# A weight-split feed-forward pair on one core: first sums issued a slab earlier, at least two product jobs between tiles of the one tile bank, column norm six quads later

## The chip, the cores and the metric

The kernel runs on one core of a Trainium2 chip, in one launch. The metric is the time of one execution in device microseconds (us); three runs were made, and the median counts. The engines of the core are TensorE (PE, with its weight loads as PEld), VectorE (DVE), ScalarE (ACT), GpSimd (POOL) and SyncE (SP), which issues most of the DMAs.

## The reference

A decoder trunk of two layers on 256 tokens of width 2048, all in float32: a layer that mixes by causal pooling, a layer of differential attention, memory cross-attention in both, and after each mixer a feed-forward part. The change lies in the two feed-forward parts alone:

```python
def squared_relu_mlp(h, w1, w2):
    z = jax.nn.relu(h @ w1)
    return (z * z) @ w2
...
x = x + squared_relu_mlp(rms_norm(x, ffn_norm[i]), w_ff1[i], w_ff2[i])
```

`w_ff1` is 2048 x 8192 and `w_ff2` 8192 x 2048.

## The kernel before, in words

**Splits.** Every weight comes from HBM as float32 and is split on chip into a high part `hi_ring` (a cast on ScalarE, L171) and a low part `lo_ring` (a subtraction on VectorE, L172); TensorE multiplies the parts and adds the products. The two rings have six slots of 512 columns. Weights in ordinary order come in *quads* of four 128x128 blocks (job N, one slot). One DMA, `raw` (L133), brings two quads.

**The planner.** `Feed` runs the program once dry to learn the order of all jobs, and lays out the weights in that order. `fill` keeps the splits up to three jobs (AHEAD) in front of TensorE, and `load` keeps the DMAs three loads in front of that, four inside the feed-forward loop. Below it, a scheduler orders each engine's instructions and each DMA queue by when it expects an instruction to be able to start, so an instruction can stand ahead of others that come earlier in the text. Every engine then works strictly in its order.

**Feed-forward part (`ffn`).** 64 *up tiles* of four quads each compute h @ w1 for 128 columns (`up_tile`, L798, on `a_part`, L406). The first four use banks `mm`, the other 60 share one PSUM bank, `x_bank`, of tag `st`. A tile ends with `evict` (L748): ScalarE copies the bank out. Then come the sum of its halves (L805), relu and square into `stage`, and the split of the result into `z`. In between, *slabs* of `w_ff2` are multiplied by a seven-product scheme on 256x1024 pieces: 56 slabs for each layer, of four *jobs* with 2, 1, 2 and 2 products (lines L844, L846, L847, into seven banks `p`). Products take `z` or sums of two `z` chunks, `sit`.

**What a slab needs.** Row A (128x1024, L139) and row B, of which only the right half is loaded (128x512, L144); B goes into a rotating row buffer for even slabs and into the one spare row for odd slabs. The *first sum* (A's left half plus B's left half) is made by DMA: the left halves of A go to one of three buffers `t1` by SyncE (L138), and B's are added in place by an accumulating DMA from GpSimd (L141), which waits for the first to land. The *K step* (L193) on VectorE subtracts B's right half from the first sum; it stands two jobs ahead of the slab's first job. L205 makes the last combination. The buffers `t1`, the spare row and others are cut from one tile, `room`, so the profile shows one name for all of them.

**What orders products and tiles.** `due` (L1035) does product jobs by a list of due times (`early`, `late`): ahead of each of the 60 tiles at least one job, then every job that is due, and inside a tile, after each quad, those that have come due.

**Norms.** After the first up tile, `rstd_from` (L477) sums the squares on TensorE into `st_x` (bank `st`, L479) and `rsqrt` (L366 to L376) makes the row form; its second last step on VectorE, `rs_t` (L375, helper line L316), is the last to read the bank. Then `columns` (L484) makes the column form with four small matmuls into the same bank (`tc_x`, L488), and ScalarE squares the row form (L803). The column form is used when the left half of the output is closed, the row form in the down tiles.

Of the kernel before, what the change touches and what calls it, by code (L numbers as in the profile page):

```python
# [12 lines left out]
AF = mybir.ActivationFunctionType  # L13
ALU = mybir.AluOpType
# [9 lines left out]
NH = 725  # L24
NBLK = 5796
SLOTS, AHEAD, LOADS, KOFF, RAWS = 6, 3, 3, 2, 4
CN = 0.5 ** (1.0 / 3.0)
LNC = math.log(CN)

# [68 lines left out]
class Feed:  # L98
# [21 lines left out]
    def load(self, upto):  # L120
        while self.lp < min(upto, len(self.plan.loads)):
            r = self.plan.loads[self.lp]
            h = self.plan.row[r]
            n = 1024
            if r[0] == "N":
                n = min(1024, (self.plan.npos - 8 * r[1]) * P)
                t = self.wpool.tile([P, 1024], F32, tag="raw", bufs=RAWS, name=f"raw{h}")
            elif r[2] and r[1] % 2:
                t = self.spare
            else:  # L130
                t = self.rows.tile([P, 1024], F32, tag="rows", bufs=3, name=f"slab{h}")
            if r[0] == "N":
                self.nc.sync.dma_start(t[:, 0:n], self.wst[h, :, 0:n])  # L133
            elif r[2] == 0:
                t1 = r[1] % len(self.t1)
                assert self.t1_of[t1] is None
                self.t1_of[t1] = r[1]
                self.nc.sync.dma_start(self.t1[t1], self.wst[h, :, 0:512])  # L138
                self.nc.sync.dma_start(t, self.wst[h])  # L139
            else:  # L140
                self.nc.gpsimd.dma_start(  # L141
                    self.t1[r[1] % len(self.t1)], self.wst[h, :, 0:512], accum_op=ALU.add
                )
                self.nc.sync.dma_start(t[:, 512:1024], self.wst[h, :, 512:1024])  # L144
            self.raw[r] = t
            self.lp += 1

    def order(self, one, other):

        self.tc.add_manual_dep(  # L150
            one.ins, other,
            mybir.DependencyInfo(
                mybir.DependencyClass.NoSync, mybir.DependencyReason.SCHED_ONLY
            ),
        )
# [123 lines left out]
def program(ctx, tc, plan, dry, xT, memT, par, lam, cst, wst, yT):  # L279
    nc = tc.nc  # L280
# [15 lines left out]
    def at(d, fn, rank=1):  # L296
        pend.setdefault(now[0] + d, []).append((rank, fn))
# [11 lines left out]
    def vt(name):  # L309
        return tp.tile([P, T], F32, tag="v", bufs=6, name=name)  # L310
# [4 lines left out]
    def stt(out, a, s, b, op0, op1, **kw):  # L315
        return nc.vector.scalar_tensor_tensor(  # L316
            out=out, in0=a, scalar=s, in1=b, op0=op0, op1=op1, **kw
        )
# [47 lines left out]
    def rsqrt(out, mean):  # L366
# [8 lines left out]
        stt(t2, mean, EPS, t, ALU.add, ALU.mult)  # L375
        stt(out, t2, 3.0 * CN * CN, h, ALU.subtract, ALU.mult, reverse0=True)  # L376

    def rsqrt_cols(out, v, parts=None):


        n = v.shape[-1]
        w = [tp.tile([P, 16], F32, tag="w8", bufs=8, name="rc")[:, :n] for _ in range(4)]
        if parts:
            for t in range(2):
                x, s, b = parts(t)
                nc.scalar.activation(w[0][:, t : t + 1], x, AF.Ln, scale=s, bias=b)
        else:
            nc.scalar.activation(w[0], v, AF.Ln)
        nc.scalar.activation(w[1], w[0], AF.Exp, bias=lnc, scale=-0.5)
        nc.vector.tensor_mul(w[2], w[1], w[1])  # L390
        nc.vector.tensor_mul(w[3], w[2], v)  # L391
        stt(out, w[3], 3.0 * CN * CN, w[1], ALU.subtract, ALU.mult, reverse0=True)

    def stat(name):
        return pp.tile([P, T], F32, tag="st", bufs=1, name=name)
# [10 lines left out]
    def a_part(ps, w, l, n, ks, xs, first=True, last=True, between=None):  # L406


        ks = list(ks)
        i = 0  # L410
        while i < len(ks):
            if between:
                between(i)
            two = []
            for k in ks[i : i + 2 - feed.pos % 2]:
                two.append((i, k % NK, *feed.block((w, l, k, n, 1))))
                feed.used()
                i += 1
            for c, k, hi, lo in two:
                nc.tensor.matmul(ps, hi, xs[:, k, :], start=first and c == 0, stop=False)  # L420
            for c, k, hi, lo in two:
                nc.tensor.matmul(  # L422
                    ps[:, T : 2 * T], lo, xs[:, k, 0:T], start=False,
                    stop=last and c == len(ks) - 1,
                )
            if feed.pos % 4 == 0:
                tick()
# [49 lines left out]
    def rstd_from(name):  # L477
        st = stat("st_" + name)
        nc.tensor.matmul(st, ones_d, acc[name], start=True, stop=True)  # L479
        r = cp.tile([P, T], F32, tag="r_" + name, name="r_" + name)  # L480
        rsqrt(r, st)
        return r

    def columns(name):  # L484

        st = stat("tc_" + name)
        for i in range(2):
            nc.tensor.matmul(  # L488
                st[:, 2 * i : 2 * i + 2], acc[name][:, i * P : i * P + P], ones_d[:, 0:2],
                start=True, stop=True,  # L490
            )
        v = tp.tile([P, 2], F32, tag="m2", bufs=12, name="cv")
        nc.vector.tensor_scalar_add(v, st[:, 0:4].rearrange("p (a b) -> p a b", b=2)[:, :, 0], EPS)
        col = cp.tile([P, 2], F32, tag="c_" + name, name="c_" + name)
        rsqrt_cols(col, v)
        col2 = cp.tile([P, 2], F32, tag="d_" + name, name="d_" + name)
        nc.vector.tensor_mul(col2, col, col)
        return col, col2
# [218 lines left out]
    def ffn(l, xs, tags, done):  # L717
# [20 lines left out]
        r = []  # L738
# [6 lines left out]
        def evict(ps):  # L745
            x = outs[cnt[0] % 2]
            cnt[0] += 1
            nc.scalar.copy(x, ps)  # L748
            return x
# [48 lines left out]
        def up_tile(i, ps, between=None):  # L798
            a_part(ps, "w_ff1", l, i, range(NK), xs, between=between)
            if i == 0:  # L800
                r.append(rstd_from("x"))
                r.append(columns("x")[1])
                nc.scalar.activation(r[0], r[0], AF.Square)  # L803
            y = evict(ps)[:, 0 : 2 * T]
            at(1, lambda: nc.vector.tensor_add(y[:, 0:T], y[:, 0:T], y[:, T : 2 * T]))  # L805
            at(2, lambda: nc.scalar.activation(y[:, 0:T], y[:, 0:T], AF.Relu))  # L806

            def square():
                nc.scalar.activation(stage[i % 8], y[:, 0:T], AF.Square)
                at(1, lambda: convert(i))  # L810

            at(2, square, 2)
# [21 lines left out]
        def bank():  # L834
            return pp.tile([P, 512], F32, tag="st", bufs=1, name="x_bank")
# [79 lines left out]
        left = {}  # L915
# [95 lines left out]
        def one_job():  # L1011
            s, j = jobs.pop(0)
            g, i, again = slabs[s]
            end = s + 1 == len(slabs) or slabs[s + 1][0] != g
            if j == 0:
                runs[s] = slab_jobs(g, i, again, end)
            runs[s](j)
            if end and s + 1 < len(slabs):
                if g == 1 and i == 23:
                    at(1, lambda: close_left(j))  # L1020
                else:
                    at(2, lambda: swap(j, 1 - g))
# [4 lines left out]
        def tiles_at(s):  # L1027

            if s < 13:
                return early[s]  # L1030
            if s >= 48:
                return late[s - 48]
            return early[12] + (s - 12) * (late[0] - early[12]) / 36

        def due(tiles, least=0):  # L1035
            n = 0
            while len(jobs) > 16:
                s, j = jobs[0]
                if tiles_at(s) + j * (tiles_at(s + 1) - tiles_at(s)) / 4 > tiles and n >= least:
                    break  # L1040
                one_job()
                n += 1

        for i in range(4):
            up_tile(i, mmt("ff1"))
# [1 line left out]
        feed.loads_ahead = 4  # L1047

        for i in range(4, 64):
            due(i, 1)  # L1050
            if turns:
                turn_left(turns.pop(0))
                due(i, 1)
            up_tile(i, bank(), lambda b, i=i: due(i + b / 16) if b > 0 and b % 4 == 0 else None)
# [104 lines left out]
    for i in range(2):  # L1159
        c = slice(2 * i, 2 * i + 2)  # L1160
# [34 lines left out]
    for i in range(2):  # L1195
        c = slice(2 * i, 2 * i + 2)
        at(5, lambda i=i, c=c: turn_rows(rows0, 2 * i, mq0[:, c, :], mqg0, mq_lo[:, c, :]))
    for h in range(4):
# [3 lines left out]
            lambda mb, h=h: [x[:, mb, h * P : h * P + P] for x in (mv, mv_lo)],  # L1202
# [185 lines left out]
    for i in range(2):  # L1388
        c = slice(2 * i, 2 * i + 2)
# [114 lines left out]
    for c in range(3):  # L1504
# [5 lines left out]
        for i in range(2):  # L1510
# [3 lines left out]
            for g in range(2):  # L1514
                h = 2 * i + g
# [7 lines left out]
    for h in range(4):  # L1523
        ps = mmt("mq1")
        x = ps[:, 0:T]
        if h < 3:
            a_part(ps, "w_in", 1, 12 + h, range(NK), x_mx)
            x = vt("mq_x")
            nc.scalar.copy(x, ps[:, T : 2 * T])
            nc.vector.tensor_add(x, ps[:, 0:T], x)  # L1530
        else:
# [4 lines left out]
            lambda mb, h=h: (mv1[:, mb, h * P : h * P + P], mv1_lo[:, h, mb, :]),  # L1536
# [94 lines left out]
```

## Time and profile before

| what | us |
|---|---|
| three timed runs | 2055.82, 2063.38, 2067.07 |
| median | 2063.38 |
| the profiled execution, its own time | 2058.8 |
| its span, first to last instruction | 2057.0 |

The profile is of one execution. Its first part gives each engine's busy time and share of the span. In a row of the timeline stand the start, the length, engine, line, operation, out<-in, shapes and count, and in brackets the idle time of the engine before it and who ended it. Rows of waits read: engine, tile and line that waited, who released it, us in total, times, longest. Matmuls are pipelined: one of 512 columns is shown as about 0.39 us long, but the next starts 0.23 us later, so distances between starts tell TensorE's pace.

### The profile page before, as it was taken

The numbers are of one execution on the slowest core, as the hardware profiler recorded it, in microseconds if no ns is written. First come the engines' busy times: TensorE is split into PE (matmuls) and PEld (weight loads), VectorE is DVE, ScalarE is ACT, GpSimd is POOL, SyncE is SP. The second block draws the span as 40 slices with busy tenths as digits, with TensorE's granted clock in tenths as the row PEclk, the third lists the DMA queues.
The fourth block names the chain that finished last, engine by engine and source line by source line (L and its number), as shares of the span: only waits on it lengthen the run. The fifth ranks groups of instructions, "written<-read, shape, count | busy, mean of one in ns | idle before, by whom it ended". The sixth has DMA issues, their size and how long they took to land.

```text
span 2057.0 us, 31770 instructions
## 1 busy us (share of the span) xinstructions
PE 2017.2 (98%) x10534; PEld 1702.6 (83%) x10534; DVE 1760.9 (86%) x3089; ACT 1501.2 (73%) x2791; POOL 149.9 (7%) x179
## 2 busy tenths in 40 slices
PE   9999989999999999999999999989999999999999
PEld 8888878888878788888888888878888887877888
DVE  8888768988989899899765798968988999888987
ACT  7765567787877868778655698557787878867765
POOL 0002200000000000000000000410000000000000
PEclk9999999999999999999999999999999999999999
DMA  8555666777777777755666544567777777766764
GB/s 315 166 198 187 202 168 218 225 220 217 227 209 233 216 219 214 207 185 186 194 225 195 166 135 141 193 170 212 228 219 224 220 232 213 220 211 189 226 208 138
DMA packets 142724, 420.08 MB, mean 204 GB/s; under 512 B 16096, under 2 KB 18784, under 8 KB 142560
## 3 DMA queue, kind: packets, MB, share of 16 engines
q1 hardware_dynamic: 126288, 388.69, 57.6%
q0 software_dynamic: 16128, 29.37, 8.8%
q8 instruction: 82, 1.34, 0.3%
q14 instruction: 82, 0.67, 0.1%
q10 hardware_dynamic: 144, 0.01, 0.0%
HBM read 415.90 MB, written 2.10 MB: 203 GB/s over the span
## 4 chain that ended last, share of the span: by engine, by line
PE 89%; DMA 3%; DVE 3%; ACT 3%; issue 1%; DVEq 0%; POOL 0%; SPq 0%; ACTq 0%
PE x_bank L420 21%; PE x_bank L422 11%; PE p L847 8%; PE p L844 8%; PE p L846 8%; PE wo L420 6%; PE wo L422 3%; DVE lo_ring L172 2%; PE u L420 2%; DMA room<-in_w 2%; PE ff L420 2%; ACT hi_ring L171 1%; DMA slab<-in_w 1%; PE u L422 1%; PE q L454 1%; PE q L456 1%
## 5 line engine op out<-in xcount | busy, mean ns | idle before, releaser
L171 ACT CAST hi_ring<-raw 128x512 fp32r<-128x512 f32 x1001 | 614.5, 620 | 281.4 <-PE x_bank L420 75.5
L172 DVE TENSOR_TENSOR lo_ring<-raw,hi_ring 128x512 fp32r<-128x512 f32 x1001 | 687.0, 694 | 113.7 <-ACT hi_ring L171 103.0
L420 PE MATMUL x_bank<-fx,hi_ring 128*128 128x512 f32 x1920 | 606.8, 397 | 2.0 <-ACT room L748 2.0
L422 PEld LDWEIGHTS x_bank<-fx,lo_ring 128*128 128x128 f32 x1920 | 361.5, 188 | 84.0 <-DVE lo_ring L172 1.7
L172 DVE TENSOR_TENSOR lo_ring<-slab,hi_ring 128x1024 fp32r<-128x1024 f32 x280 | 340.5, 1221 | 58.6 <-ACT hi_ring L171 55.2
L422 PE MATMUL x_bank<-fx,lo_ring 128*128 128x256 f32 x1920 | 378.8, 279 | 0.8 <-DVE lo_ring L172 0.8
L171 ACT CAST hi_ring<-slab 128x1024 fp32r<-128x1024 f32 x280 | 292.4, 1048 | 101.5 <-PE x_bank L420 60.8
L420 PEld LDWEIGHTS x_bank<-fx,hi_ring 128*128 128x128 f32 x1920 | 318.1, 189 | 45.6 <-ACT room L748 18.2
L847 PE MATMUL p<-lo_ring,sit 128*128 128x512 f32 x448 | 177.0, 396 | 12.8 <-DVE lo_ring L172 12.5
L141 POOL DMA_DIRECT2D room<-in_w x112 | 96.9, 868 | 1183.5 <-DMA room<-in_w 1163.1
L844 PE MATMUL p<-hi_ring,sit 128*128 128x512 f32 x448 | 177.5, 396 | 1.3 <-ACT hi_ring L171 1.3
L846 PE MATMUL p<-hi_ring,sit 128*128 128x512 f32 x448 | 175.9, 393 | 0.0
L420 PE MATMUL wo<-cat,hi_ring 128*128 128x512 f32 x512 | 161.8, 397 | 0.3 <-DVE rc L391 0.3
L171 ACT CAST hi_ring<-room 128x512 fp32r<-128x512 f32 x168 | 128.5, 765 | 38.1 <-PE p L846 15.6
L172 DVE TENSOR_TENSOR lo_ring<-room,hi_ring 128x512 fp32r<-128x512 f32 x168 | 144.8, 862 | 1.9 <-ACT hi_ring L171 1.9
L847 PE MATMUL p<-lo_ring,z 128*128 128x512 f32 x336 | 132.0, 393 | 3.7 <-DVE lo_ring L172 3.7
L844 PE MATMUL p<-hi_ring,z 128*128 128x512 f32 x336 | 132.0, 393 | 0.2
L846 PE MATMUL p<-hi_ring,z 128*128 128x512 f32 x336 | 131.8, 392 | 0.0
L847 PEld LDWEIGHTS p<-lo_ring,sit 128*128 128x128 f32 x448 | 84.2, 188 | 37.1 <-DVE lo_ring L172 21.4
L422 PEld LDWEIGHTS wo<-cat,lo_ring 128*128 128x128 f32 x512 | 95.9, 188 | 22.0
L422 PE MATMUL wo<-cat,lo_ring 128*128 128x256 f32 x512 | 101.5, 279 | 0.0
L806 ACT ACTIVATE room<-room 128x256 f32<-128x256 f32 x128 | 53.5, 418 | 62.6 <-DVE room L805 62.2
(374 smaller groups left out, 3415.5 us busy)
## 6 DMA issues: line engine op xcount, KB each, us to landing
raw<-in_w SPq DMA_DIRECT2D x500, 512.0 KB, 4.2
slab<-in_w SPq DMA_DIRECT2D x112, 512.0 KB, 4.3
room<-in_w SPq DMA_DIRECT2D x168, 256.0 KB, 3.3
room<-in_w POOLq DMA_DIRECT2D x112, 256.0 KB, 5.9
slab<-in_w SPq DMA_DIRECT2D x56, 256.0 KB, 4.5
memraw<-in_mem SPq DMA_DIRECT2D x5, 512.0 KB, 4.5
resid<-in_x SPq DMA_DIRECT2D x8, 256.0 KB, 5.4
out_y<-resid SPq DMA_DIRECT2D x16, 128.0 KB, 1.9
```

The costliest lines, as they stand in the source:

```text
L141: self.nc.gpsimd.dma_start(self.t1[r[1] % len(self.t1)], self.wst[h, :, 0:512], accum_op=ALU.add)
L171: self.last_cast = self.nc.scalar.copy(hi, src)
L172: low = self.nc.vector.tensor_sub(lo, src, hi.bitcast(F32))
L420: nc.tensor.matmul(ps, hi, xs[:, k, :], start=first and c == 0, stop=False)
L422: nc.tensor.matmul(ps[:, T : 2 * T], lo, xs[:, k, 0:T], start=False, stop=last and c == len(ks) - 1,)
L454: nc.tensor.matmul(ps[t], x[t][1], hi, start=k == 0, stop=False)
L456: nc.tensor.matmul(ps[t], x[t][0], lo, start=False, stop=k == NK - 1)
L806: at(2, lambda: nc.scalar.activation(y[:, 0:T], y[:, 0:T], AF.Relu))
L844: nc.tensor.matmul(ps, a[1], hi, start=new, stop=False, **again)
L846: nc.tensor.matmul(ps, a[0], hi, start=False, stop=False, **again)
L847: nc.tensor.matmul(ps, a[0], lo, start=False, stop=end, **again)
```

## The change

Three edits. The load of a slab's row A no longer issues its own first sum but the next slab's, both halves at once (the first slab of each layer issues its own too), and the load of row B issues none. `due` does at least two jobs ahead of each of the 60 tiles. The column form and the square of the row form are put off by six ticks, and a tick is one quad.

```diff
+PER_PART = 56
...
             elif r[2] == 0:
-                t1 = r[1] % len(self.t1)
-                assert self.t1_of[t1] is None
-                self.t1_of[t1] = r[1]
-                self.nc.sync.dma_start(self.t1[t1], self.wst[h, :, 0:512])
+                if r[1] % PER_PART == 0:
+                    self.first_sum(r[1])
                 self.nc.sync.dma_start(t, self.wst[h])
+                if (r[1] + 1) % PER_PART:
+                    self.first_sum(r[1] + 1)
             else:
-                self.nc.gpsimd.dma_start(
-                    self.t1[r[1] % len(self.t1)], self.wst[h, :, 0:512], accum_op=ALU.add
-                )
                 self.nc.sync.dma_start(t[:, 512:1024], self.wst[h, :, 512:1024])
...
+    def first_sum(self, n):
+        i = n % len(self.t1)
+        assert self.t1_of[i] is None
+        self.t1_of[i] = n
+        left, right = (self.wst[self.plan.row["S", n, c], :, 0:512] for c in range(2))
+        self.nc.sync.dma_start(self.t1[i], left)
+        self.nc.gpsimd.dma_start(self.t1[i], right, accum_op=ALU.add)
...
                 r.append(rstd_from("x"))
-                r.append(columns("x")[1])
-                nc.scalar.activation(r[0], r[0], AF.Square)
+                at(6, lambda: r.append(columns("x")[1]))
+                at(6, lambda: nc.scalar.activation(r[0], r[0], AF.Square))
...
         for i in range(4, 64):
-            due(i, 1)
+            due(i, 2)
             if turns:
                 turn_left(turns.pop(0))
                 due(i, 1)
```

## The prediction

> **What bounds the kernel now.** I read the page's first part, then TensorE's own waits, then the timeline at the longest of them, and last who waits for each of the DMAs that the change moves. Durations come from one profiled execution: 2058.8 us, of which the span is 2057.0; it lies 4.6 us under the median of the three timed runs, 2063.38 (2055.82 to 2067.07).
>
> ```profile
> PE 2017.2 (98%) x10534; PEld 1702.6 (83%) x10534; DVE 1760.9 (86%) x3089; ACT 1501.2 (73%) x2791; POOL 149.9 (7%) x179
> ```
>
> TensorE is busy 2017.2 us of 2057.0. Unless matmuls go away (none does), the most that any reordering can win is the idle 40 us, about 5 of them at the two ends of the span, and what matmuls lose at half clock. TensorE's waits name where that is (us in total, times, longest):
>
> ```profile
> PE p L847 <- DVE lo_ring L172: 16.1, 15, 3.6
> PE tc_x L488 <- DVE rs_t L316: 13.5, 2, 7.0
> PE x_bank L420 <- ACT room L748: 2.0, 4, 0.7
> ```
>
> Three rows, and the three parts of the change stand one against each: the column norm's matmuls (`tc_x`), the slab weights' low halves, the tile bank. But a row says who released TensorE, not why the releaser was late, so each has to be followed back.
>
> **Part 1, the column norm six quads on.** In layer 0:
>
> ```profile
> 257.02 0.60 PE L479 MATMUL st_x<-acc,ones_d 128*128 128x256 f32 x2
> 257.27 0.81 PE L420 MATMUL ff<-fx,hi_ring 128*128 128x512 f32 x2
> ...
> 258.85 0.63 PE L420 MATMUL ff<-fx,hi_ring 128*128 128x512 f32 x2
> ...
> 259.55 0.62 PE L420 MATMUL ff<-fx,hi_ring 128*128 128x512 f32 x2
> ...
> 264.71 0.69 DVE L193 TENSOR_TENSOR slab<-room,slab 128x512 f32<-128x512 f32 x1 [6.04 <-DMA room<-in_w]
> ...
> 265.82 0.69 DVE L193 TENSOR_TENSOR room<-room 128x512 f32<-128x512 f32 x1 [0.42 <-DMA room<-in_w]
> 266.43 0.42 DVE L316 SCALAR_TENSOR_TENSOR rs_t<-st_x,rs_t 128x256 f32<-128x256 f32 x1
> ...
> 266.90 1.01 PE L488 MATMUL tc_x<-ones_d,acc 128*128 128x2 f32 x4 [6.50 <-DVE rs_t L316]
> ...
> 267.77 1.20 PE L420 MATMUL ff<-fx,hi_ring 128*128 128x512 f32 x2
> ...
> 272.98 0.64 PE L420 MATMUL ff<-fx,hi_ring 128*128 128x512 f32 x2
> ```
>
> Read it backwards. `tc_x` shares bank `st` with the row norm's `st_x`, so it waits until `rs_t` (L316) has read that bank. `rs_t` stands on VectorE behind the first two K steps (L193), and the first of these waits 6.04 us for the accumulating load of the first sum. After `st_x` TensorE had four pairs of blocks to do, at 0.70 each (258.85 to 259.55), and then stood 6.50 us. Layer 1 is the same picture, 6.97 us, and it ends at the first K step too:
>
> ```profile
> 1354.03 0.81 PE L420 MATMUL ff<-fx,hi_ring 128*128 128x512 f32 x2
> ...
> 1361.32 0.69 DVE L193 TENSOR_TENSOR slab<-room,slab 128x512 f32<-128x512 f32 x1 [5.88 <-DMA room<-in_w]
> ...
> 1364.14 1.01 PE L488 MATMUL tc_x<-ones_d,acc 128*128 128x2 f32 x4 [6.97 <-DVE rs_t L316]
> 1365.01 1.20 PE L420 MATMUL ff<-fx,hi_ring 128*128 128x512 f32 x2
> ...
> 1368.81 0.63 PE L420 MATMUL ff<-fx,hi_ring 128*128 128x512 f32 x2
> ```
>
> The idle time is not the whole price. In windows (us, PE busy, then PEclk) the clock stays halved after each stop:
>
> ```profile
> 266.90:272.90 6.00, 6.00 (x20) 0.50 0.58 136
> 1364.10:1368.60 4.50, 4.46 (x15) 0.51 0.72 154
> 1812.40:1815.30 2.90, 0.02 (x1) 1.00 0.28 110
> 1815.70:1819.10 3.40, 3.40 (x12) 0.50 0.44 154
> ```
>
> Four pairs from 267.77 to 272.98 took 5.21 us instead of 4 x 0.70: 2.4 lost. Three from 1365.01 to 1368.81 took 3.80 instead of 2.10: 1.7 lost. So this stop costs 6.5 + 7.0 + 2.4 + 1.7 = **17.6 us**. [...]
>
> Does the stop go, or does it only move? The first K step still blocks VectorE for those 6 us, and now TensorE runs on meanwhile. By the instruction order of the changed program, VectorE has split the weights of six quads (twelve pairs) before the first K step, and `tc_x` now stands exactly after those twelve pairs. So TensorE gets there at 257.27 + 12 x 0.70 = 265.7. On VectorE `rs_t` now follows the first K step directly; the second has moved behind two more splits. From 264.71, with 0.61 between starts (265.82 to 266.43), `rs_t` starts at 265.3 and ends at 265.75: TensorE waits 0.1 us. In layer 1: 1354.03 + 8.4 = 1362.4, against 1361.32 + 0.61 + 0.42 = 1362.35, no wait. What is late next is the low half of the seventh quad, which has to wait for VectorE too: after `rs_t` come a small add, `r_x` and the split, at most 0.42, 0.42 and 0.69, so 267.3 at the latest; TensorE, after four `tc_x` matmuls (under 1.0) and two high-half matmuls (0.47), wants it at 267.2. That is even. I take 0.2 us of new wait in both layers together, bounds 0 and 7.4: the third sum's first half now runs beside the first accumulating loads, and if they land 2 us later in each layer TensorE stops that long, with 1.7 of slow clock. The chain of waits has two of these loads (start, us), the page the median of all:
>
> ```profile
> 257.65 8.14 DMA room<-in_w
> ...
> 1354.07 8.97 DMA room<-in_w
> ```
>
> ```profile
> room<-in_w POOLq DMA_DIRECT2D x112, 256.0 KB, 5.9
> ```
>
> **Saved: 17.4 us.** ScalarE's columns step, which stood behind `tc_x`, moves along and nobody needs its result before the left half is closed.
>
> **Part 2, first sums a slab earlier.** Who waited for the accumulating load (first two rows), and who for the slab's second load on L144 (last two):
>
> ```profile
>   DVE slab L193: 11.9, 2
>   DVE room L193: 1.5, 2
> ```
>
> ```profile
>   DVE room L193: 29.5, 24
>   DVE slab L193: 19.1, 13
> ```
>
> The name `room` hides two buffers: the sums and the spare row are both cut from it. The accumulating load is waited for four times, at the first two slabs of each layer. All other 37 waits at K, 48.6 us, are for L144, which this part doesn't touch. And the load that it does touch is already as early as its three buffers allow:
>
> ```profile
> SPq L138 <- DVE lo_ring L172: 196.3, 84, 6.4
> SPq L144 <- DVE lo_ring L172: 191.1, 79, 4.7
> ```
>
> The queue holds L138 until a split has read its buffer (84 times), since the scheduler puts loads in order of when they can start, not of the text. So in the changed SP order the fourth first-sum load stands at place 123 instead of 125, then 130 for 131, 137 for 138, 144 for 146, and from the eighth slab on at the same place (151, 156, 161). GpSimd issues the same 112 accumulating loads in the same order, each when its left half lands. No DMA is added. **Value: 0.** For the two first slabs nothing can be earlier: they start when the old tile in that room is free.
>
> **Part 3, two jobs between tiles.** The row for weight loads and one turn:
>
> ```profile
> PEld x_bank L420 <- ACT room L748: 18.7, 70, 1.1
> ```
>
> ```profile
> 660.84 0.39 PE L844 MATMUL p<-hi_ring,sit 128*128 128x512 f32 x1
> ...
> 661.07 0.69 PE L420 MATMUL x_bank<-fx,hi_ring 128*128 128x512 f32 x2
> 661.60 0.40 PE L422 MATMUL x_bank<-fx,lo_ring 128*128 128x256 f32 x2
> 661.83 0.63 PE L420 MATMUL x_bank<-fx,hi_ring 128*128 128x512 f32 x2
> 662.30 0.39 PE L422 MATMUL x_bank<-fx,lo_ring 128*128 128x256 f32 x2
> ```
>
> Only the weight load waits for the copy out of the bank, and it overlaps: this pair takes 0.53 to the next row instead of 0.47. At 0.06 to 0.10 each, 70 turns cost 4 to 7 us; I take 5.6. A second job puts at least 0.69 us more TensorE work (three matmuls, each 0.23 to the next as from 660.84 to 661.07) in front, seven times that delay, so it goes: **saved 5.6**, bounds 0 and 18.7 (all of it exposed). The four real stops (2.0 us) are at the bank swaps and stay.
>
> The same edit bunches the work. In the TensorE orders, runs of three or more products between weight blocks rise from 48 to 126. A two-wide slab split takes VectorE 1.22 us
>
> ```profile
> L172 DVE TENSOR_TENSOR lo_ring<-slab,hi_ring 128x1024 fp32r<-128x1024 f32 x280 | 340.5, 1221 | 58.6 <-ACT hi_ring L171 55.2
> ```
>
> while its two products take TensorE 6 x 0.23 = 1.38, so a run by itself can be fed; what a run shortens is the distance between the split that frees a buffer of L144 and the K step that wants the new load. Priced by the durations of the VectorE instructions between them, that distance is under 3 us at 14 slabs before and at 8 after, under 4 at 32 and 31. The shortest move: from slab 52 (1.4 us) to slabs 21 (1.0) and 13 (1.4) of each layer. So K still waits about as often, elsewhere. VectorE's 48.6 us there cost TensorE 16.1, plus twice 1.7 of slow clock. **Value 0**, bounds -12 and +15.
>
> **Sum:** 2058.8 - 17.4 - 5.6 = 2035.8 on the profiled base, 2040.4 on the median. I predict **2038 us**.
>
> **Rivals.**
> - *The stop moves to the first splits (12%).* The sums' loads land 2 us later because a third one runs beside them. For: they are the slow ones already, 8.14 and 8.97 us against a median of 5.9. Against: the load whose place it takes in the queue is also of 256 KB. 2038 + 7.4 = 2045.
> - *New K waits (13%).* Slabs 13 and 21 of each layer stop TensorE like the worst one, 2.9 + 1.7 us, while only half of the old stops go: +18.4 - 9.8 = about +9, and up to +15: 2047 to 2053.
> - *The queue gains (7%).* L144 comes earlier since the sums are out of its way; half to all of 16.1 + 3.4 goes: 2018 to 2028.
> - *Slower (6%).* The runs empty the six-slot ring just ahead of each K step, so VectorE's K waits pass to TensorE whole: 48.6 - 16.1 = 32.5 more, and 1.7 of slow clock at some six of them (two had it, and the sum is three times as long), +43: 2081. It decides once a run of three or more products ends right before a K step that waits. Against: VectorE is busy 45.75 of 50 us at 650 to 700, so there is little, but some, room to catch up.
>
> ```profile
> 650.00:700.00 50.00, 50.00 (x256) 41.90 (x255) 45.75 (x68) 40.60 (x72) 3.45 (x4) 1.00 0.79 226
> ```
>
> **How the numbers follow.** Forecast 62%, 2030 to 2045. The range 2024 to 2053 takes in the later loads, most of the new K waits and half of the queue's gain. 0.5%, about what a measurement of this kernel can tell from no change, is 10 us: under 2053 is faster. Forecast, first rival, queue and most of the second give 0.87; the rest of the second 0.07; the slower rival 0.06.
>
> **What would show it.** The wait of `tc_x` falls from 13.5 to under 1 and the half-clock stretches at both places go; the first K step still waits some 6 us. The 18.7 of the tile bank falls under 3. Accumulating loads past the second slab are still never waited for. Waits of L847 stay between 8 and 25 us, at other slabs, 13 and 21 among them. I am wrong if L172 stops TensorE right after `tc_x`, or if L847's waits pass 30.

## The result and the profile after

| | before | after |
|---|---|---|
| median, us (four runs each) | 2061.65 (2055.82 to 2067.07) | 2028.97 (2023.32 to 2032.30) |
| span of the profiled execution | 2057.0 | 2021.6 |

The ratio is 0.9839, 95% interval 0.9803 to 0.9876: about 33 us faster (26 to 41). The forecast was 2038, 23 to 25 us faster, with a range of 2024 to 2053. So sign and range held, and some 9 us of the gain were not forecast: 2029 lies just under the 2030 to 2045 to which the prediction gave 62%. The profiled execution after is the fastest of the four, 2023.32, so its rows show a little less than the median loses. Line numbers of the changed kernel are six higher than before (L172 is L178, L193 is L199, L847 is L853); row B's load L144 is L142, the accumulating load L141 is L152.

The page's first part after, and TensorE's waits (us in total, times, longest):

```profile
PE 1999.2 (99%) x10534; PEld 1702.0 (84%) x10534; DVE 1756.0 (87%) x3089; ACT 1495.9 (74%) x2791; POOL 149.9 (7%) x179
```

```profile
PE p L853 <- DVE lo_ring L178: 12.8, 11, 2.1
PE p L850 <- ACT room L754: 2.5, 2, 2.3
PE p L850 <- ACT hi_ring L177: 1.1, 1, 1.1
```

The row of `tc_x` (13.5) is gone, and so is the bank's among the matmul waits. Its row among the weight loads fell from 18.7 in 70:

```profile
PEld x_bank L426 <- ACT room L754: 0.5, 2, 0.3
```

The place of the first stop, in time order:

```profile
264.73 0.69 DVE L199 TENSOR_TENSOR slab<-room,slab 128x512 f32<-128x512 f32 x1 [6.12 <-DMA room<-in_w]
...
265.81 0.61 PE L494 MATMUL tc_x<-ones_d,acc 128*128 128x2 f32 x4
...
266.32 0.42 ACT L809 ACTIVATE r_x<-r_x 128x256 f32<-128x256 f32 x1 [5.05 <-DVE r_x L322]
...
276.21 0.50 PE L850 MATMUL p<-hi_ring,z 128*128 128x512 f32 x1 [1.10 <-ACT hi_ring L177]
...
277.47 0.50 PE L853 MATMUL p<-lo_ring,z 128*128 128x512 f32 x1 [0.53 <-DVE lo_ring L178]
```

The first K step waits as before, 6.12 us; `tc_x` starts with no bracket, so nothing was waited for. But ScalarE, too, works in order: it stands 5.05 us before it squares `r_x`, the row form, although this step was put off. And TensorE stops ten microseconds later, at the first product jobs. In layer 1 as well, there behind ScalarE's copy of a tile:

```profile
1358.82 0.58 ACT L754 COPY room<-ff 128x512 f32<-128x512 f32 x1
...
1359.44 0.50 PE L850 MATMUL p<-hi_ring,sit 128*128 128x512 f32 x1 [2.25 <-ACT room L754]
```

Both places in windows (us, PE busy, PEld, DVE, ACT, POOL, PEclk, DMA share, GB/s), before and then after:

```profile
250.00:300.00 50.00, 43.50 (x229) 37.57 (x229) 32.96 (x63) 29.02 (x57) 5.32 (x6) 0.90 0.63 180
1350.00:1400.00 50.00, 43.03 (x229) 36.95 (x228) 33.95 (x63) 30.20 (x61) 5.16 (x6) 0.93 0.63 179
```

```profile
250.00:300.00 50.00, 48.15 (x264) 40.59 (x263) 37.14 (x71) 33.05 (x65) 6.17 (x7) 1.00 0.70 199
1350.00:1400.00 50.00, 47.75 (x257) 40.73 (x256) 44.92 (x83) 38.59 (x72) 2.60 (x3) 1.00 0.70 209
```

TensorE's idle time there fell from 6.50 + 6.97 to 1.85 + 2.25, and the clock no longer halves: granted 0.90 and 0.93 of full speed before, 1.00 after. With the 4.1 us of slow clock that the prediction worked out: 17.6 before, 4.1 after, 13.5 saved.

Next, what VectorE's K step waited for. `slab` are the even slabs (row B in a rotating buffer), `room` the odd ones (spare row), here with the first sums. Before, then after:

```profile
  DMA room<-in_w: 42.8, 28
  DMA slab<-in_w: 19.1, 13
```

```profile
  DMA room<-in_w: 37.8, 21
  DMA slab<-in_w: 4.6, 6
```

Without the first sums, `room` fell from 29.5 to 25.9. So the even slabs' wait has nearly gone, and the odd ones' fell little. These are single profiles, and the odd ones' wait differs much between them: over the kernels below that leave these K steps where they were, 20.3 to 32.4 us with one job between tiles and 18.2 to 25.9 with two. The even ones' is clear of that, 18.1 to 24.3 with one job and 2.2 to 4.9 with two. That is what the prediction had at zero; the experiments show what it is worth.

### The profile page after: what moved, and what is told of

It is laid out like the page before. It is cut to its first block, busy times and chain, and to the rows that moved or that the text cites. A ratio compares the mean times of both kernels' runs of the same rounds, so it can differ in the third digit from the quotient of the medians.

```text
span 2021.6 us, 31855 instructions
## 1 busy us (share of the span) xinstructions
PE 1999.2 (99%) x10534; PEld 1702.0 (84%) x10534; DVE 1756.0 (87%) x3089; ACT 1495.9 (74%) x2791; POOL 149.9 (7%) x179
## 4 chain that ended last, share of the span: by engine, by line
PE 91%; DVE 3%; DMA 3%; ACT 2%; issue 1%; DVEq 0%; ACTq 0%
PE x_bank L426 22%; PE x_bank L428 11%; PE p L853 8%; PE p L850 8%; PE p L852 8%; PE wo L426 6%; PE wo L428 3%; DMA room<-in_w 3%; PE u L426 2%; DVE lo_ring L178 2%; PE u L428 1%; PE q L460 1%; PE q L462 1%; PE k L460 1%; PE q L461 1%; PE v L462 1%
## 5 line engine op out<-in xcount | busy, mean ns | idle before, releaser
L178 DVE TENSOR_TENSOR lo_ring<-raw,hi_ring 128x512 fp32r<-128x512 f32 x1001 | 681.6, 693 | 107.9 <-ACT hi_ring L177 96.2
L426 PE MATMUL x_bank<-fx,hi_ring 128*128 128x512 f32 x1920 | 600.7, 394 | 0.0
L178 DVE TENSOR_TENSOR lo_ring<-slab,hi_ring 128x1024 fp32r<-128x1024 f32 x280 | 340.9, 1220 | 51.5 <-ACT hi_ring L177 48.9
L426 PEld LDWEIGHTS x_bank<-fx,hi_ring 128*128 128x128 f32 x1920 | 313.8, 189 | 22.7
L853 PE MATMUL p<-lo_ring,sit 128*128 128x512 f32 x448 | 175.6, 393 | 12.1 <-DVE lo_ring L178 11.9
L152 POOL DMA_DIRECT2D room<-in_w x112 | 96.9, 868 | 1144.9 <-DMA room<-in_w 1128.3
L178 DVE TENSOR_TENSOR lo_ring<-room,hi_ring 128x512 fp32r<-128x512 f32 x168 | 144.6, 861 | 9.0 <-ACT hi_ring L177 8.9
L853 PE MATMUL p<-lo_ring,z 128*128 128x512 f32 x336 | 131.3, 391 | 0.8 <-DVE lo_ring L178 0.8
L853 PEld LDWEIGHTS p<-lo_ring,sit 128*128 128x128 f32 x448 | 84.0, 188 | 36.5 <-DVE lo_ring L178 18.5
L850 PEld LDWEIGHTS p<-hi_ring,sit 128*128 128x128 f32 x448 | 83.9, 187 | 12.9 <-ACT room L754 3.3
```

The source lines that it names most:

```text
L152: self.nc.gpsimd.dma_start(self.t1[i], right, accum_op=ALU.add)
L178: low = self.nc.vector.tensor_sub(lo, src, hi.bitcast(F32))
L850: nc.tensor.matmul(ps, a[1], hi, start=new, stop=False, **again)
L853: nc.tensor.matmul(ps, a[0], lo, start=False, stop=end, **again)
```

## The experiments

Each kernel ran beside the kernel before on the same chip, and four kernels of a group shared one.

| kernel | median, us | kernel before there | ratio (95%) |
|---|---|---|---|
| `c_only` | 2045.06 | 2060.25 | 0.9921 (0.9895 to 0.9947) |
| `f_only` | 2054.73 | 2060.25 | 0.9971 (0.9949 to 0.9993) |
| `d_only` | 2036.40 | 2060.25 | 0.9887 (0.9861 to 0.9913) |
| `k0_behind` | 2041.57 | 2060.25 | 0.9914 (0.9887 to 0.9941) |
| `k_late` | 2025.14 | 2056.14 | 0.9846 (0.9821 to 0.9870) |
| `d_k_late` | 2017.35 | 2056.14 | 0.9813 (0.9790 to 0.9837) |
| `c_and_d` | 2025.53 | 2056.14 | 0.9851 (0.9827 to 0.9875) |
| `after_k0_behind` | 2018.42 | 2056.14 | 0.9820 (0.9796 to 0.9843) |
| `k_even_late` | 2043.51 | 2058.36 | 0.9937 (0.9916 to 0.9958) |
| `k_odd_late` | 2032.85 | 2058.36 | 0.9883 (0.9854 to 0.9912) |
| `all_k_late` | 2002.37 | 2058.36 | 0.9732 (0.9704 to 0.9760) |
| `k_late_d_k0` | 2002.92 | 2058.36 | 0.9734 (0.9706 to 0.9762) |

Differences below are those of the medians on the same chip; half an interval is some 5 us.

### The three parts alone

**`c_only`, the column norm later and nothing else.**

```diff
-                r.append(columns("x")[1])
-                nc.scalar.activation(r[0], r[0], AF.Square)
+                at(6, lambda: r.append(columns("x")[1]))
+                at(6, lambda: nc.scalar.activation(r[0], r[0], AF.Square))
```

> Only the column norm is put off by six quads. Theory (the stop at tc_x is VectorE standing at the first K steps, and twelve pairs of blocks cover it): the 17.6 us of the two stops go but for a rest, since in this order both K steps still stand ahead of rs_t: TensorE reaches tc_x at 265.7 and rs_t ends at 266.9 in layer 0, 1.7 us late in layer 1, so 14 to 15 us less than before. Rival (the stop only moves to the next splits): 0 to 5 us less, with L172 stopping TensorE within 10 us after st_x.

Measured: 15.2 us less. TensorE's waits:

```profile
PE p L847 <- DVE lo_ring L172: 21.5, 19, 3.6
PE tc_x L488 <- DVE rs_t L316: 2.2, 2, 1.6
```

The stop at `tc_x` goes but for 2.2 us, and this part has about the worth that it was given. (The low halves' row is larger than before, 16.1, but the profiled execution, 2055.83, is the longest of this kernel's eight, 10.8 us over their median.)

**`f_only`, the first sums a slab ahead and nothing else** (`load` and `first_sum` as in the diff of the change):

```diff
+                if r[1] % PER_PART == 0:
+                    self.first_sum(r[1])
                 self.nc.sync.dma_start(t, self.wst[h])
+                if (r[1] + 1) % PER_PART:
+                    self.first_sum(r[1] + 1)
```

> Only the first sums are issued a slab earlier. By the SyncE order only the third sum's load and the second slab's row B change places, and the second K step moves behind rs_t; later slabs stand as before. Theory (nobody waits for a first sum past the second slab): the two stops at tc_x end 1.1 and 1.8 us sooner, so about 3 us less, and the K waits for L144 stay at 48.6 us. Rival (the earlier sums relieve the queue and so the K steps): 10 us or more less, with the K waits under 35 us.

Measured: 5.5 us less, interval 1.4 to 10.5. The row of `tc_x`:

```profile
PE tc_x L494 <- DVE rs_t L322: 11.3, 2, 5.9
```

Each of the two stops is about 1 us shorter, since the second K step no longer stands ahead of `rs_t`. The interval leaves room for more than that. K's waits for row B, which the theory left at 48.6, were 38.4 in the profile, the even slabs' 18.1 and the odd ones' 20.3; but the odd ones' lie inside the spread between profiles, and the profiled execution, 2046.24, is the shortest of twelve. So whether the sums relieve the queue a little is open here.

**`d_only`, two jobs between tiles and nothing else.**

```diff
         for i in range(4, 64):
-            due(i, 1)
+            due(i, 2)
```

> Only the two jobs between tiles. Theory (the gain beyond the forecast, some 12 us, is this part's: turns of the bank covered, worst K waits moved to places where more splits are in stock): 14 to 20 us less than before, x_bank waiting for L748 gone, K waits for L144 near 30 us instead of 48.6. Rival (only the turns are covered): 5 to 7 us less, K waits unchanged in sum.

Measured: 23.9 us less, four times the 5.6 of the forecast and above this expectation too. Its rows: TensorE's waits, the bank's turns, and K's waits.

```profile
PE tc_x L488 <- DVE rs_t L316: 11.8, 2, 6.0
PE p L847 <- DVE lo_ring L172: 9.6, 7, 2.0
```

```profile
PEld x_bank L420 <- ACT room L748: 0.5, 2, 0.3
```

```profile
  DMA room<-in_w: 30.7, 17
  DMA slab<-in_w: 3.8, 5
```

The turns went as forecast; with them went the even slabs' K waits (19.1 to 3.8). The odd ones' fell too, from 29.5 to 18.9 (the row has the first sums besides). Slab 52 of layer 0 shows how: the issue of its row B and its K step, in the kernel before and then in `d_only`.

```profile
865.06 0.33 SPq L144 DMA_DIRECT2D slab<-in_w  x1
870.45 0.69 DVE L193 TENSOR_TENSOR slab<-room,slab 128x512 f32<-128x512 f32 x1 [4.21 <-DMA slab<-in_w]
```

```profile
854.75 0.33 SPq L144 DMA_DIRECT2D slab<-in_w  x1
861.28 0.68 DVE L193 TENSOR_TENSOR slab<-room,slab 128x512 f32<-128x512 f32 x1
```

Before, K's turn came 870.45 - 4.21 - 865.06 = 1.2 us behind the issue, and the load took over 5 (K started 5.39 behind the issue). With two jobs between tiles, other VectorE work stands in between, K's turn comes 6.5 us behind the issue, and it waits for nothing.

### The head of the line at the first K step

**`k0_behind`**: the kernel before, columns in place, with the first two K steps of each layer ordered on VectorE behind the row norm's last step.

```diff
-                self.gate = None
+                if p[1] % 56:
+                    self.gate = None
...
+                if not dry:
+                    feed.gate = norm_done[0].ins.name
```

> The kernel before, with the first two K steps of each layer ordered behind the row norm's last step on VectorE; the column norm stays where it was. Theory (tc_x waits because rs_t stands behind a K step that waits for its load): the stops go without moving tc_x, 15 to 18 us less. Rival (the shared bank and the chain of the row norm themselves take the time): the stop stays at 3 us or more in each layer, less than 8 us gained.

Measured: 18.7 us less, and no row of `tc_x` in the waits of TensorE's matmuls. So the stop was the first K step's place ahead of `rs_t`, as the prediction read it backwards.

**`after_k0_behind`**: the same edit on the changed kernel.

> The whole change, and the first K step of each layer ordered behind the row norm's last VectorE step. Theory (with the change, the first K step's 6 us block on VectorE comes back 10 us later as the stops of the first product jobs, 1.10 and 0.53 us in layer 0, 2.25 in layer 1): those stops fall under 1 in sum, 3 to 4 us less than the whole change, 2023 to 2026. Rival (VectorE is late there for its amount of work, not for the block): the stops stay, within 1 us of the whole change.

Measured: 37.7 less than before, where the whole change has 32.7: 5 us, which the intervals of the two ratios alone don't tell from none. The windows do:

```profile
250.00:300.00 50.00, 49.71 (x276) 42.44 (x275) 40.38 (x76) 35.45 (x69) 6.18 (x7) 1.00 0.72 216
1350.00:1400.00 50.00, 49.63 (x266) 42.31 (x265) 44.81 (x80) 39.37 (x73) 2.60 (x3) 1.00 0.67 210
```

The idle 1.85 + 2.25 of the changed kernel shrinks to 0.29 + 0.37. The stops at the first product jobs were the rest of the same block: columns later lets TensorE run on meanwhile, and VectorE and ScalarE come to the product jobs late.

### The K steps of the other slabs

**`k_late`**: the kernel before, with K steps held back to where the text has them. In the two traces SP issues its loads in the same order, and TensorE's matmuls stand in the same order but for 92 of 10534, in a few places; what moves is K, and what stands around it on VectorE and ScalarE.

```diff
         low = self.nc.vector.tensor_sub(lo, src, hi.bitcast(F32))
+        self.low = low
...
             one = sub(rb[:, 0:512], t1, rb[:, 512:1024])
+            if p[1] % 56:
+                self.order(one, self.low.ins.name)
```

> The kernel before, with every K step (the first of each layer excepted) put on VectorE behind the weight split that stands last ahead of it in the text, instead of where the scheduler hoists it. The orders of TensorE and of SP's queue stay as before; only K moves: by the durations of the VectorE instructions between, no K comes less than 6.1 us behind the split that lets its load start (before, 70 of 108 came less than 5 behind). Theory (K comes before the slab's second load has landed, and this is where the time of the stage goes): the K waits for that load, 48.6 us before, fall under 5; L847's waits from 16.1 to under 5; the half-clock stretches late in layer 1 go; with 2 to 3 us from the first stops of tc_x, since the second K step goes behind rs_t, 18 to 23 us less: about 2040. Rival (a K wait only shifts slack, and TensorE is late because of the splits' pace): K's waits go, but L847's stay above 10; 3 to 6 us less: about 2056.

Measured: 31.0 less, as much as the whole change, and above the theory's 18 to 23. (By the durations of the VectorE instructions between, 48 of the 108 K steps stood less than 5 us behind before, not 70; with K late the nearest stands 6.2 behind.) One stop of the kernel before, followed from the issue of row B to TensorE:

```profile
1807.74 0.33 SPq L144 DMA_DIRECT2D room<-in_w  x1
...
1811.98 0.39 PE L844 MATMUL p<-hi_ring,z 128*128 128x512 f32 x1
1813.40 0.69 DVE L193 TENSOR_TENSOR room<-room 128x512 f32<-128x512 f32 x1 [3.22 <-DMA room<-in_w]
1814.01 2.35 DVE L172 TENSOR_TENSOR lo_ring<-slab,hi_ring 128x1024 fp32r<-128x1024 f32 x2
...
1815.28 0.19 PEld L847 LDWEIGHTS p<-lo_ring,sit 128*128 128x128 f32 x1 [3.34 <-DVE lo_ring L172]
1815.28 0.50 PE L847 MATMUL p<-lo_ring,sit 128*128 128x512 f32 x1 [2.91 <-DVE lo_ring L172]
```

And the same slab with K late: K starts 11 us behind the issue, and waits for nothing.

```profile
1787.17 0.33 SPq L144 DMA_DIRECT2D room<-in_w  x1
...
1798.54 0.68 DVE L194 TENSOR_TENSOR room<-room 128x512 f32<-128x512 f32 x1
```

The waits of the weight loads show every such stop, before and then with K late; the third row is K's own waits with K late (the first sums of both layers are left):

```profile
PEld p L847 <- DVE lo_ring L172: 27.9, 30, 4.1
```

```profile
PEld p L850 <- DVE lo_ring L172: 0.8, 2, 0.4
```

```profile
  DMA room<-in_w: 12.4, 2
```

Neither row is the time that TensorE lost. In the stop above, the next matmul was due 0.23 us after the one at 1811.98 and started 3.07 later than that. The matmuls' row has 2.91, 0.16 too little, since a matmul's modelled end reaches into the gap; it shows short stops not at all. The weight loads' row has 3.34, 0.27 too much. With 0.27 off each of the 30, 27.9 comes to about 20 us; the matmuls' row, 16.1 in 15, which the prediction took, comes to 18.5 with 0.16 added to each, without the short stops.

So late K steps took away about 20 us of stops at the low halves, 3.4 of slow clock late in layer 1 (before, twice 3.4 us at 0.50, from 1815.7 and from 1863.5; with K late, 1.00 over 1812 to 1820 and 1860 to 1868), about 2 at `tc_x` (13.5 to 11.6), and the four stops at the bank swaps, which the prediction left standing (2.0 by the matmuls' row, 2.6 by the same sum). That makes 28 of the 31.0 measured; the rest is inside the interval (27 to 37).

**`k_even_late`** and **`k_odd_late`**: the same order for the K steps of the even slabs alone, or of the odd ones.

The even slabs' edit, against `k_late` (the odd ones' has `== 1`):

```diff
-            if p[1] % 56:
+            if p[1] % 56 > 1 and p[1] % 2 == 0:
```

> The kernel before, with the K steps of the even slabs alone (from the third on) behind the weight split that stands last ahead of them; TensorE's and SP's orders stay. The late K steps of all slabs saved 31 us, about 3 of it at tc_x. Theory (due 2 saved its time beyond the turns by the lead of the even slabs' K: their waits fell from 17.8 to 3.0 there, those of the odd ones only from 27.0 to 17.5): the even waits go here, the odd ones stay near 27, and 12 to 18 us are saved: about 2043. Rival (the odd slabs' waits, the larger sum, are those that stop TensorE): less than 8 us: about 2052.

> The same for the odd slabs alone (from the fourth on). Theory: the rest of the 28, 10 to 16 us: about 2043. Rival (the odd waits stop TensorE): 20 or more: about 2034. Third case (a wait taken away only makes the next K come sooner and wait longer): the even slabs' waits grow past 25, and less than 8 us are saved.

Measured: 14.9 less (interval 9 to 17) and 25.5 less (18 to 30). The first is as expected. The second is the rival's: the odd waits, the larger sum, cost TensorE more. The two add up to 40, more than the 31 of both together; with the odd waits gone, the even ones remain (19.2, 15) and TensorE loses little to them, a weight-load wait of 9.9 in 16 instead of 27.9 in 30, by the sum above some 6 us instead of 20:

```profile
  DMA slab<-in_w: 19.2, 15
```

```profile
PEld p L850 <- DVE lo_ring L172: 9.9, 16, 1.4
```

So a wait of VectorE costs TensorE only a part, and that part depends on the other waits. That the splits' lead covers the rest, and that waits close together use up the same lead, would explain it; no run shows it apart.

**`d_k_late`**: the edits of `k_late` and `d_only` together.

> The late K steps and due 2 together, the rest as before. Theory (due 2 saves the tile turns, 5.6 us, with 2 at the bank swaps, and the rest of the 24 us that it saved alone came from K's waits, which are already gone here): 5 to 9 us less than the late K steps alone, 26 to 30 less than before: about 2032. Rival (two jobs between tiles save by themselves, through work for TensorE while a split is late): the whole 24 comes on top, or at least 15 more than the late K steps alone.

Measured: 7.8 us less than `k_late` on the same chip. The bank's row in `k_late` and in `d_k_late`:

```profile
PEld x_bank L423 <- ACT room L751: 16.5, 72, 0.3
```

```profile
PEld x_bank L423 <- ACT room L751: 0.4, 2, 0.2
```

Once K no longer stands too early, two jobs between tiles are worth the turns of the bank, 5.6 by the prediction, or little more. The other 16 us that the edit saved alone came through K.

### The sum of the parts, and a faster kernel

**`c_and_d`**: the edits of `c_only` and `d_only`, so the change without its first sums.

> The whole change without its first part, the sums loaded a slab ahead. Theory (the sums have a worth only while tc_x stops, by the second K step's place): within 4 us of the whole change, so about 29 to 37 us less than before: 2024 to 2032. Rival (parts add up, and the third sum's loads cost the whole change some 6 us): 39 less, about 2021. A second rival (the sums bring 5.5 here as they did alone): 27 less, about 2034.

Measured: 30.6 less; the whole change 32.7, ratios 0.9851 and 0.9839. No difference shows, so the sums have no worth in the pair, or less than can be told here.

**`all_k_late`**: the whole change with the edits of `k0_behind` and of `k_late`. **`k_late_d_k0`**: the kernel before with the edits of `k0_behind`, `k_late` and `d_only`, so the same without the later columns and the earlier sums.

> The whole change, the first K step behind the row norm's last VectorE step, and every other K step behind the split that stands last ahead of it: every loss named so far taken away. If they are independent: the late K steps with due 2, 38.5 less than before, and the two places of tc_x, 11.1 us of stops with 2 to 4 of slow clock: about 52 less, 2004 to 2008, with no row of K, tc_x or the tile bank left among TensorE's waits. Rival (the first product jobs then stop instead, or TensorE outruns the splits): 40 to 45 less, 2011 to 2016.

> The same without the change's first and third part: columns in place and sums as before, so due 2, the first K step behind the row norm and the other K steps late. Theory (columns later and earlier sums only work around the K steps' waits, and have no worth of their own once these are gone): within 3 us of the version that has them. Rival (the columns' place has a worth of its own): 5 us or more above it.

Measured: 56.0 and 55.4 less, 2002.4 and 2002.9 us, some 22 under the whole change by the ratios, and 4 more than the sum of 52 that was expected of the first. The largest row among TensorE's waits in the first:

```profile
PE p L857 <- ACT hi_ring L177: 1.0, 2, 0.5
```

No K step, no `tc_x` and no bank is left there. And the later columns and earlier sums, worth 15 and some 5 us alone, together make 0.6 us here: both only worked around K steps that stood too early on VectorE. The times also differ less from one execution to the next: on this chip, 16 executions of the kernel before lie between 2045.35 and 2065.78, the six of `all_k_late` between 2002.21 and 2003.50. So most of the spread went with these waits too.

## Why the prediction was right or wrong

**Part 1: mechanism right, 4 us too much.** Forecast 17.4, saved 13.5; `c_only` alone 15.2. Of the three steps behind it, `tc_x` after twelve pairs without a wait, the first K step still waiting 6 us, and the end of both slow stretches, all are in the rows. The mis-sized term is the new wait, taken at 0.2 with bounds 0 and 7.4, which measured 4.1. I looked for what is late next only up to the seventh quad's split. The block came back further on, at the first product jobs, through ScalarE: it waited 5.05 us for `r_x`, and a cast and a copy of a tile behind that were late. `after_k0_behind` takes these stops away.

**Part 2: value 0, and 0 in the pair.** After the change the accumulating loads are waited for at the first slab of each layer alone (before, at the first two), and never past the second, as forecast:

```profile
  DVE slab L199: 11.9, 2
```

What `f_only` saves is at least partly a place in VectorE's order (the second K step behind `rs_t`), which the prediction had read in the order of the changed kernel and priced under part 1.

**Part 3, the bank's turns: right.** Forecast 5.6, measured 7.8 with K out of the way; the row of 18.7 fell to 0.5. The 2.0 at the swaps went as well, which the prediction had left standing; `k_late` loses them without the second job, so they hang on K.

**Part 3, K's waits: the step that failed.** "So K still waits about as often, elsewhere" was priced at 0, bounds -12 and +15. In the pair, 32.7 less 13.5 and 7.8 leaves about 11 for it. Two things were wrong with the step.

- *The threshold.* I counted K steps less than 3 and 4 us behind the split that frees the buffer, all slabs together. The page of before has the landing times of row B for the even slabs, and of the spare row and the sums together:

```profile
slab<-in_w SPq DMA_DIRECT2D x56, 256.0 KB, 4.5
```

```profile
room<-in_w SPq DMA_DIRECT2D x168, 256.0 KB, 3.3
```

 With a median of 4.5, the even slabs must be counted at 5 or 6. The same distances, counted under 5.5: of 54 even slabs 21 before and 6 after; of 54 odd ones 35 and 40. The even slabs' waits fell (19.1 to 4.6) and the odd ones' little (29.5 to 25.9). `k_even_late` puts 9 to 17 us on taking away all 19.1, so some 11 for 14.5 fits.
- *The price.* I took 16.1 us of TensorE time for all K waits, from the matmuls' row, and 3.4 of slow clock; `k_late` shows about 29 (31.0 less 2 at `tc_x`), since that row is some 4 us short and the stops at the bank swaps belong to K too. The rival "the queue gains", 2018 to 2028, was sized from it. It came near to what happened in time, but not in cause: L144 did not come earlier since the sums were out of its way, as `c_and_d` shows, but K came later behind it. That the range held is thus partly luck: its lower end, 2024, was half of that rival.

The new stops that the second rival feared are there, at the slabs it named. The one at slab 13 of layer 1:

```profile
1503.92 0.69 DVE L199 TENSOR_TENSOR room<-room 128x512 f32<-128x512 f32 x1 [2.36 <-DMA room<-in_w]
...
1505.80 0.51 PE L853 MATMUL p<-lo_ring,sit 128*128 128x512 f32 x1 [1.87 <-DVE lo_ring L178]
```

By the matmuls' rows the four stops at slabs 13 and 21 are 1.52, 1.14, 1.87 and 1.38 us, 5.9 in sum, where the rival had 18.4 with the slow clock; none halves the clock, which is 1.00 in the 3.4 us behind each. The 1.7 of slow clock that bounds and rivals add to every stop of 2 to 3 us (in 7.4, 18.4 and the slower rival's 43) is shown by no run as a price of every such stop: behind 2.86 us in `c_only` and 2.25 and 2.09 in the changed kernel the clock was 1.00, behind 2.91 in the kernel before it was 0.50, and behind 2.17 in `c_only` 0.61 over 4.3 us. The stops that went were more: the weight loads' wait for low halves fell from 27.9 in 30 to the row below. With 0.27 off each, that is from 20 to 15 us; with the 3.4 of slow clock and the 2.6 at the bank swaps it makes between 10 and 11, near the 11 above, as far as two profiles can tell.

```profile
PEld p L853 <- DVE lo_ring L178: 20.7, 20, 2.5
```

The slower rival, runs of products that empty the ring, didn't happen: L853's waits are 12.8, inside the 8 to 25 that were named. (In the traces the runs of three or more products, counted by their first matmuls, rise from 40 to 124, not from 48 to 126; nothing else in the prediction hangs on that.) No run took away the stops at slabs 13 and 21 alone.

## What to carry to other kernels

When an engine works strictly in its order, look for the instruction that waits for a DMA while others behind it could run (here the first K step, 6.04 us, with `rs_t` behind it), and move that one back: one rule of order did as much as three edits that worked around it (31.0 us and 32.7). Before counting which waits a reordering takes away, take the threshold from the landing time of that very load, class by class, and price a TensorE stall by the distances between the starts of matmuls, since here the matmuls' row of waits had 16 us and the weight loads' row 28 for what was about 20.

## What the runs showed of the hardware

In these traces the length of a stop alone doesn't tell whether the clock halves. In `c_only` TensorE stopped 2.86 us before 716.08, and only 1.56 us before `tc_x` at 267.14:

```profile
716.08 0.50 PE L847 MATMUL p<-lo_ring,sit 128*128 128x512 f32 x1 [2.86 <-DVE lo_ring L172]
```

```profile
267.14 0.38 PE L488 MATMUL tc_x<-ones_d,acc 128*128 128x2 f32 x2 [1.56 <-DVE rs_t L316]
```

```profile
267.70:271.00 3.30, 3.30 (x11) 2.77 (x11) 3.30 (x7) 2.67 (x6) 0.00 (x0) 0.50 0.89 225
716.10:719.50 3.40, 3.40 (x17) 2.88 (x18) 3.40 (x5) 2.29 (x4) 0.00 (x0) 1.00 0.41 157
```

The longer one left the clock (the column 1.00) alone, the shorter one was followed by half clock (0.50). In the kernel before, the stops of 2.91 and 3.62 us that end at 1815.28 and 1862.41 were followed by half clock too, 0.50 over 1815.7 to 1819.1 and over 1863.5 to 1866.9; in the changed kernel the longest ones, 2.25 us to 1359.44 and 2.09 to 1853.77, were followed by 1.00. What decides beside the length was not shown. The prediction's 1.7 for stops of 2 to 3 us was too much for some and right for others.
